# Four small re-timings in a fused encoder layer: early operands one token tile later, first rows in a larger slot, two products on VectorE, and a staggered last product

## The chip, the core and the metric

The kernel runs on one core of a Trainium2 chip. Its five engines are TensorE (PE: matrix products into the banks of PSUM), VectorE (DVE), ScalarE (ACT), GpSimd (POOL) and SyncE (SP, which here issues the DMA transfers). Each engine works through its own queue in order, and a semaphore holds an instruction until what it needs is there. The metric is the time on the device of one execution, in microseconds (us). A measurement of this kernel can tell a difference of about 0.2%, which is 3.6 us.

## What is computed

One layer of a streaming encoder, on 1024 tokens of width 1024 in float32. Two attention branches, a cross-attention to 256 memory tokens and a SwiGLU block follow one another, and each adds its result to the token rows. The change touches the end of the cross-attention and everything behind it:

```python
x = x + memory_cross_attention(hc, mn, w_cq[layer], w_ckv[layer], w_co[layer])
hf = rmsnorm(x, norm_ffn_g[layer])
g, u = jnp.split(hf @ w_gate_up, 2, axis=-1)          # 1024 -> 2 x 2816
x = x + (jax.nn.silu(g) * u) @ w_down                  # 2816 -> 1024
return rmsnorm(x, norm_final_g)
```

## The kernel before

**Arithmetic.** A float32 operand is split into a high part (a cast on ScalarE) and a low part (a subtraction on VectorE); the method `split` of the class does both. Each product is three matmuls: high by high, low by high and high by low (`prod`, or lines 217 to 219 in the part ahead of it).

**Token tiles and rows.** The 1024 tokens are eight tiles of 128. `last_half` takes token tiles 4 to 7 through the output projection of the cross-attention: `add_out` is a group of 12 matmuls and then one VectorE addition to the rows (line 634), twice for each tile, once for each half of the columns; `last_rms` squares and scales the rows (lines 108, 101, 103, 110), and `norms` transposes what the tile before left on TensorE (line 791) and copies it into `hq` (line 794). Between the two groups of tile 4, `ff.before()` starts the SwiGLU block's operands: `mov_early` splits four quarters of the token operand into tiles `T` (lines 894 and 895).

**SwiGLU.** The block multiplies two-by-two blocks of its matrices by a scheme with seven products in place of eight; their order is 1, 2, 6, 5, 7, 3, 4 (`ORDER`). Products 1, 6, 7 and 4 accumulate in bank "a", 2 in "d", and 5 and 3 in "c". The 22 feature tiles of gate (g) and up (u) go in pairs, which gives 154 items of 12 matmuls. Pairs t0 and t1 share the start: items 0 to 7 are products 1 and 2 of t0 g, t0 u, t0 g, t0 u and then the same of t1; items 8 to 17 are products 6, 5, 7, 3 and 4 of t0; items 18 and 19 are product 6 of t1 g and t1 u, which needs t1's bank "a" to have been read. These reads of items 4 to 7 are held back in a list `later` and are flushed after item 17. `make` prepares an item's weights four items ahead (`AHEAD`): on GpSimd sums and differences of weight blocks (lines 956 to 960), then the split. `read` copies a bank into rows `r` (ScalarE, line 989) or adds it to them (VectorE, line 991). `after` adds silu on ScalarE (lines 1021 to 1025) and the products of gate and up rows on GpSimd (line 1029, 128x1024, and line 1033, 128x512).

**Slots.** On-chip tiles come out of rings by tag. A new tile waits until the oldest of its ring is no longer used: "row" has 3 slots of 4 KB for each partition, "sum" 2 of 4 KB, "hidden" and "four" share 8 of 8 KB, "combo" has 3 of 8 KB.

**Down product.** `down` runs 77 steps (7 products by 11 feature pairs), each 12 matmuls: 3 for each of four token tiles. `down_load` asks for a step's operands 8 steps ahead, and `down_make` splits them (`do`) 2 steps ahead. At a product's last step the four banks are added to the rows `xr` (line 1172). At products 3 (steps 55 to 65) and 4 (steps 66 to 76) a row is then complete: two squares on ScalarE (line 1176, both halves of the row), three small operations on GpSimd (lines 1178 to 1180), two scalings on VectorE into `fin` (line 1144), and the output's DMA (line 1146).

The order within an engine's queue is set by a scheduler that works from the program's order and its own estimates, except where `keep_in_program_order` stands.

Of the kernel before, what the change touches and what calls it, by code (L numbers as in the profile page):

```python
# [12 lines left out]
ALU = mybir.AluOpType  # L13
AX = mybir.AxisListType

P = 128
# [21 lines left out]
def build(tc, x, mem, wqk, wv, wg, wup, wout, wcq, wck, wcv, wco, wgu, wdn,  # L38
# [530 lines left out]
    with tc.tile_pool(name="late", bufs=1, reuse_waits="tile") as lt:  # L569
# [66 lines left out]
        def add_out(*a):  # L636
            for _ in out_steps(*a):
                pass
# [175 lines left out]
        def last_half():  # L814

            ws = [[unit(wco[4 + cc + 2 * i], home=t1_tile if cc else None) for i in range(2)] for cc in range(2)]
            for tt in range(4, 8):
                add_out(o_sta(2), ws[0], 4, 0, tt)
                if tt == 4:
                    norms(0)  # L820
                    ff.before()
                add_out(o_sta(2), ws[1], 4, 1, tt)
                norms(0)
                last_rms(tt)

# [39 lines left out]
class FeedForward:  # L865
# [44 lines left out]
        t = self.T[n, i] = self.tiles["hidden"]("T", n)  # L910
        self.split(t[:, 0], t[:, 1], src)

    def mov_early(self):
        for i in (0, 2):
            self.put(1, i, self.quad(i, 0))
        for i in (0, 2):
            self.put(2, i, self.quad(i + 4, 0))

    def mov_late(self, n):

# [17 lines left out]
    class Pair:  # L938
# [38 lines left out]
        def read(self, n):  # L977
            ff = self.ff
            acc = self.bk[ff.BANK[n]]
            if n == 1:  # L980
                self.r = [ff.tiles["sum" if self.f >= FT else "row"]("r"), None]
            elif n == 5:
                self.r[1] = ff.tiles["row"]("r")

            to = {1: (0, 0), 2: (0, 0), 6: (0, 1), 3: (0, 1), 5: (1, 1), 7: (1, 1)}.get(n)
            if to:
                r = self.r[to[0]][:, to[1]]
                if n in (1, 6, 5):
                    ff.act.copy(out=r, in_=acc)  # L989
                else:  # L990
                    ff.dve.tensor_tensor(out=r, in0=r, in1=acc, op=ALU.add)

    class Tile2:
# [19 lines left out]
        def after(self, p, n):  # L1013
            p.read(n)
            g, u, ff = self.g, self.u, self.ff
            act, dve, pool, sp = ff.act, ff.dve, ff.pool, ff.sp
            if p is g:
                if n == 1 and self.f >= 4:
                    self.down_weights()
                elif n == 7:  # L1020
                    act.activation(g.r[1][:, 1], g.r[1][:, 1], AF.Silu)
                elif n == 3:
                    act.activation(g.r[0], g.r[0], AF.Silu)
                elif n == 4:
                    act.activation(g.r[1][:, 0], g.bk["a"], AF.Silu)
            elif n == 7 and self.before:
                self.before.down_weights()
            elif n == 3:
                pool.tensor_tensor(out=g.r[0], in0=g.r[0], in1=u.r[0], op=ALU.mult)
                sp.dma_start(out=ff.a_d[self.f // 2][:, 0:2], in_=g.r[0])  # L1030
            elif n == 4:

                pool.tensor_tensor(out=g.r[1][:, 1], in0=g.r[1][:, 1], in1=u.r[1][:, 1], op=ALU.mult)
                dve.tensor_tensor(out=g.r[1][:, 0], in0=u.bk["a"], in1=g.r[1][:, 0], op=ALU.mult)
                sp.dma_start(out=ff.a_d[self.f // 2][:, 2:4], in_=g.r[1])
                t = ff.tiles["four"]("s")
                (a11, a21), (a12, a22) = ([r[:, 0], r[:, 1]] for r in g.r)
                pool.tensor_tensor(out=t[:, 2], in0=a11, in1=a21, op=ALU.subtract)
                dve.tensor_tensor(out=t[:, 0], in0=a21, in1=a22, op=ALU.add)
                dve.tensor_tensor(out=t[:, 1], in0=t[:, 0], in1=a11, op=ALU.subtract)  # L1040
                dve.tensor_tensor(out=t[:, 3], in0=a12, in1=t[:, 1], op=ALU.subtract)
                sp.dma_start(out=ff.s_d[self.f // 2], in_=t)
# [24 lines left out]
    def before(self):  # L1067

        tiles = []
        for f in range(0, FT, 2):  # L1070
            tiles.append(self.Tile2(self, f, tiles[-2] if f in (4, 6) else None))
        self.items = []
        for ns, ts in ((self.ORDER[:2], tiles[:2]), (self.ORDER[2:], tiles[:2]), (self.ORDER, tiles[2:])):
            for t in ts:
                self.items += t.items(ns)
        self.loaded = []
        self.mov_early()
        for i in range(2):
            self.make(i)

    def run(self, last_norm):
        with self.tc.tile_pool(name="fps", bufs=1, space=bass.MemoryType.PSUM, reuse_waits="tile") as self.fps:
            later = []
            self.steps = [(n, j) for n in self.ORDER for j in range(FT // 2)]
            self.raws, self.ops = {}, {}
            for i in range(2, AHEAD):
                self.make(i)
            for i, (t, p, n) in enumerate(self.items):
                if i == 2:
                    last_norm()  # L1090
                if i in LATE:
                    self.mov_late(LATE[i])
                self.make(i + AHEAD)
                if i == len(self.items) - 9:
                    for k in range(4):
                        self.down_load(k)
                if i == len(self.items) - 2:
                    self.down_make(0)
                p.mm(n)

                if i < 8 and t is self.items[4][0]:
                    later.append((t, p, n))
                else:
                    t.after(p, n)
                if n == 4 and p is t.u:
                    while later:
                        t, p, n = later.pop(0)
                        t.after(p, n)
            self.down()
# [14 lines left out]

    def down_make(self, i):
        if i < len(self.steps):
            t = self.tiles["combo"]("do")
            self.split(t[:, 0], t[:, 1], self.raws[i])
            self.ops[i] = t[:, 0], t[:, 1]

    def down(self):
        act, dve, pool, sp = self.act, self.dve, self.pool, self.sp
        LOADS, MADE = 8, 2
        for i in range(4, LOADS):
            self.down_load(i)
        self.down_make(1)
# [2 lines left out]
        bks = {}  # L1139
        fin = []  # L1140

        def finish(row, o):
            for c in range(2):
                self.tc.keep_in_program_order(dve.scalar_tensor_tensor(
                    out=o[:, c], in0=xs[row][:, c], scalar=sf[:, row, 1:2], in1=gbc[:, c], op0=ALU.mult, op1=ALU.mult))
                sp.dma_start(out=self.out[row * P:(row + 1) * P, c * HALF:(c + 1) * HALF], in_=o[:, c])

        for i, (n, j) in enumerate(self.steps):
            self.down_load(i + LOADS)
            self.down_make(i + MADE)  # L1150
            if i == 4:
# [3 lines left out]
                    xs += [t[:, k].rearrange("p (a b) -> p a b", a=2) for k in range(2)]  # L1155
                gbc = self.tiles["row"]("gbc")
                sp.dma_start(out=gbc, in_=self.g_final.partition_broadcast(P).rearrange("p (a b) -> p a b", a=2))
            b = "a" if self.BANK[n] == "a" else "c"
            first = n in self.FIRST
            if first and j == 0:  # L1160
                bks[b] = [self.bank() for _ in range(4)]
            hi, lo = self.ops.pop(i)
            for tt in range(4):
                ts = slice(tt * P, (tt + 1) * P)
                self.prod(bks[b][tt], (hi[:, 0, ts], lo[:, 0, ts]), (hi[:, 1], lo[:, 1]), first and j == 0,
                          j == FT // 2 - 1, not first)
            if j < FT // 2 - 1:
                continue
            for tt in range(4):
                half, c = {1: (0, 0), 2: (0, 0), 6: (0, 1), 5: (1, 1), 7: (1, 1), 3: (0, 1), 4: (1, 0)}[n]  # L1170
                row = half * 4 + tt
                dve.tensor_tensor(out=xs[row][:, c], in0=xs[row][:, c], in1=bks[b][tt], op=ALU.add)
                if n in (3, 4):
                    o = self.tiles["row"]("fin")
                    for cc in range(2):
                        act.activation(o[:, cc], xs[row][:, cc], AF.Square, accum_out=sf[:, row, cc:cc + 1])
                    s0, s1 = sf[:, row, 0:1], sf[:, row, 1:2]
                    pool.tensor_tensor(out=s1, in0=s0, in1=s1, op=ALU.add)
                    pool.tensor_scalar(out=s1, in0=s1, scalar1=1.0 / D, scalar2=EPS, op0=ALU.mult, op1=ALU.add)
                    pool.tensor_tensor(out=s1, in0=s1, in1=self.mhalf, op=ALU.pow)  # L1180
                    fin.append((row, o))
                    if tt:
                        finish(*fin[-2])
                    if tt == 3:
                        finish(*fin[-1])


def _cols(w, n=128):
# [56 lines left out]
```

## Time and profile before

| | |
|---|---|
| median of 3 runs | 1800.18 us (1797.94 to 1800.35) |
| the profiled execution's own time | 1801.18 us |
| its span, first to last instruction | 1799.4 us |
| TensorE busy | 1745.7 us (97%) |
| mean granted TensorE clock | 0.993 |
| VectorE, ScalarE, GpSimd busy | 1088.5, 766.2, 519.4 us (60%, 43%, 29%) |

The span is the time from the first to the last instruction on the core; 1.8 us of the execution's own time lie around it. Clock 1.00 stands for TensorE's 2.4 GHz, 0.50 for 1.2 GHz. Matmuls overlap one another in the pipeline, so that one of 0.39 us follows the one before at a shorter distance than that.

### The profile page before, as it was taken

To read this page: it belongs to the slowest core of one execution; us is meant where nothing else is said; L and a number is where in the kernel's file an instruction comes from. 1 tells how busy PE (TensorE), PEld (TensorE's weight loads), DVE (VectorE), ACT (ScalarE), POOL (GpSimd) and SP (SyncE) were. 2 spreads that over 40 slices of the span, in tenths; PEclk is the share of its full clock that TensorE was granted. 3 is DMA by queue.
4 is the path that set the end of the run, shared out by engine and by line. 5 is a ranking of instruction groups with operands and counts; after the bars stand their busy time and mean duration, and the time that the engine had idled before them with its cause. 6 is when DMAs were issued, how large, how long until landed. Compare 5 with 4: busy or idle time off the path is not lost.

```text
span 1799.4 us, 23586 instructions
## 1 busy us (share of the span) xinstructions
PE 1745.7 (97%) x8836; PEld 1471.2 (82%) x8836; DVE 1088.5 (60%) x1495; ACT 766.2 (43%) x1425; POOL 519.4 (29%) x555
## 2 busy tenths in 40 slices
PE   7999999999999999999999999989999999999996
PEld 7778797898898888888888887778888888888885
DVE  6585666646756744445645446776676666655555
ACT  5354554535545545213542244343333333334343
POOL 3232213223323202200000001376766656400002
PEclk9999999999999999999999999999999999999998
DMA  5332313212221255421321114225644434586663
GB/s 192 104 90 68 103 42 103 71 54 62 77 74 62 83 219 214 152 72 69 131 104 49 54 63 153 94 87 196 233 177 174 164 141 187 212 286 192 195 192 117
DMA packets 75730, 229.80 MB, mean 128 GB/s; under 512 B 9184, under 2 KB 9440, under 8 KB 71776
## 3 DMA queue, kind: packets, MB, share of 16 engines
q1 hardware_dynamic: 75616, 228.30, 36.7%
q8 instruction: 69, 1.13, 0.3%
q14 instruction: 45, 0.37, 0.1%
HBM read 160.10 MB, written 55.57 MB: 120 GB/s over the span
## 4 chain that ended last, share of the span: by engine, by line
PE 64%; issue 3%; DVE 3%; ACT 1%; POOL 1%; DMA 0%; DVEq 0%; POOLq 0%; ACTq 0%
PE bk L901 11%; PE bk L902 11%; PE bk L900 10%; PE acc L217 5%; PE acc L218 5%; PE acc L219 5%; PE s L95 2%; PE s L96 2%; PE s L97 2%; PE s L217 2%; PE s L219 2%; PE s L218 2%; PE av L454 1%; PE tr L438 1%; PE av L95 0%
## 5 line engine op out<-in xcount | busy, mean ns | idle before, releaser
L217 PE MATMUL acc<-t,wsp 128*128 128x512 f32 (+1 forms) x704 | 270.4, 384 | 0.0
L219 PE MATMUL acc<-t,wsp 128*128 128x512 f32 (+1 forms) x704 | 270.3, 384 | 0.0
L218 PE MATMUL acc<-t,wsp 128*128 128x512 f32 (+1 forms) x704 | 270.2, 384 | 0.0
L900 PE MATMUL bk<-T,w 128*128 128x512 f32 x616 | 240.8, 391 | 5.2 <-ACT r L989 5.0
L901 PE MATMUL bk<-T,w 128*128 128x512 f32 x616 | 240.3, 390 | 1.3 <-DVE w L895 1.3
L902 PE MATMUL bk<-T,w 128*128 128x512 f32 x616 | 240.5, 390 | 0.5 <-DVE T L895 0.5
L895 DVE TENSOR_TENSOR w<-fr,w 128x512 fp32r<-128x512 f32 x132 | 140.8, 1099 | 72.7 <-ACT w L894 72.3
L81 DVE TENSOR_TENSOR wsp<-raw,wsp 128x1024 fp32r<-128x1024 f32 x98 | 124.0, 1265 | 67.5 <-ACT wsp L76 66.2
L219 PEld LDWEIGHTS acc<-t,wsp 128*128 128x128 f32 x704 | 133.3, 189 | 25.1
L76 ACT CAST wsp<-raw 128x1024 fp32r<-128x1024 f32 x96 | 100.7, 1049 | 124.5 <-PE s L219 50.2
L218 PEld LDWEIGHTS acc<-t,wsp 128*128 128x128 f32 x704 | 133.3, 189 | 22.8 <-DVE wsp L81 0.7
L217 PEld LDWEIGHTS acc<-t,wsp 128*128 128x128 f32 x704 | 133.3, 189 | 22.2
L895 DVE TENSOR_TENSOR do<-dr,do 128x1024 fp32r<-128x1024 f32 x77 | 96.8, 1260 | 82.9 <-ACT do L894 81.3
L900 PEld LDWEIGHTS bk<-T,w 128*128 128x128 f32 x616 | 116.1, 188 | 30.2 <-ACT r L989 5.8
L901 PEld LDWEIGHTS bk<-T,w 128*128 128x128 f32 x616 | 116.1, 188 | 25.8 <-DVE w L895 1.7
L902 PEld LDWEIGHTS bk<-T,w 128*128 128x128 f32 x616 | 116.0, 188 | 24.9 <-DVE T L895 0.9
L894 ACT CAST do<-dr 128x1024 fp32r<-128x1024 f32 x77 | 81.2, 1054 | 118.0 <-PE bk L902 103.4
L901 PE MATMUL bk<-do 128*128 128x512 f32 x308 | 120.2, 390 | 0.8 <-DVE do L895 0.8
L902 PE MATMUL bk<-do 128*128 128x512 f32 x308 | 119.9, 389 | 0.0
L900 PE MATMUL bk<-do 128*128 128x512 f32 x308 | 119.7, 389 | 0.0
L217 PE MATMUL acc<-wsp,t 128*128 128x256 f32 (+1 forms) x368 | 118.1, 321 | 1.1 <-POOL wsp L80 1.1
L219 PE MATMUL acc<-wsp,t 128*128 128x256 f32 (+1 forms) x368 | 116.5, 317 | 0.7 <-DVE wsp L81 0.7
(216 smaller groups left out, 3736.8 us busy)
## 6 DMA issues: line engine op xcount, KB each, us to landing
fr<-in_wgu SPq DMA_DIRECT2D x44, 512.0 KB, 5.7
ad<-r SPq DMA_DIRECT2D x22, 512.0 KB, 3.3
sd<-s SPq DMA_DIRECT2D x11, 1024.0 KB, 4.1
dw<-in_wdn SPq DMA_DIRECT2D x22, 512.0 KB, 5.5
wd<-dw SPq DMA_DIRECT2D x11, 1024.0 KB, 4.1
dr<-sd SPq DMA_DIRECT2D x44, 256.0 KB, 3.7
dr<-wd SPq DMA_DIRECT2D x44, 256.0 KB, 3.9
dr<-ad SPq DMA_DIRECT2D x33, 256.0 KB, 5.1
```

The source lines that it names most:

```text
L76: act.copy(out=hi, in_=src)
L81: lo_eng.tensor_tensor(out=lo, in0=src, in1=hi.bitcast(F32), op=ALU.subtract)
L95: pe.matmul(acc, lh, rh, start=(i == 0), stop=False)
L96: pe.matmul(acc, ll, rh, start=False, stop=False)
L217: pe.matmul(acc, lh, rh, start=(i == 0), stop=False)
L218: pe.matmul(acc, ll, rh, start=False, stop=False)
L219: pe.matmul(acc, lh, rl, start=False, stop=(i == n - 1))
L894: self.act.copy(out=hi, in_=src)
L895: self.dve.tensor_tensor(out=lo, in0=src, in1=hi.bitcast(F32), op=ALU.subtract)
L900: mm(acc, l[0], r[0], start=start, stop=False, skip_group_check=onto)
L901: mm(acc, l[1], r[0], start=False, stop=False, skip_group_check=onto)
L902: mm(acc, l[0], r[1], start=False, stop=stop, skip_group_check=onto)
```

## The change

It has four parts. **(1)** `mov_early` is split: product 1's two operand tiles are made where all four were, in `ff.before()`, and product 2's two are made a token tile later, after tile 5's second `add_out`. **(2)** Rows r of pair t1's gate take an 8 KB "four" slot in place of a "row" slot, and the held-back reads of t1 are flushed after item 15 in place of item 17. **(3)** For pair t0 alone the products of lines 1029 and 1033 run on VectorE, not on GpSimd. **(4)** The end of the down product: the last 4 operands come from "hidden" slots (of the ring "t1"), the last 5 steps run token tile by token tile (15 matmuls for a tile, then its row's end) in place of step by step, a half of a row is squared as soon as that half is complete, and the scaled rows overwrite `xr` and leave from there.

```diff
                 add_out(o_sta(2), ws[1], 4, 1, tt)
+                if tt == 5:
+                    ff.mov_early(2)
                 norms(0)
...
-    def mov_early(self):
+    def mov_early(self, n):
         for i in (0, 2):
-            self.put(1, i, self.quad(i, 0))
-        for i in (0, 2):
-            self.put(2, i, self.quad(i + 4, 0))
+            self.put(n, i, self.quad(i + (0 if n == 1 else 4), 0))
...
-                self.r = [ff.tiles["sum" if self.f >= FT else "row"]("r"), None]
+                tile = ff.tiles["four"]("r")[:, :2] if self.f == 2 else ff.tiles["sum" if self.f >= FT else "row"]("r")
+                self.r = [tile, None]
...
-                pool.tensor_tensor(out=g.r[0], in0=g.r[0], in1=u.r[0], op=ALU.mult)
+                (pool if self.f else dve).tensor_tensor(out=g.r[0], in0=g.r[0], in1=u.r[0], op=ALU.mult)
...
-                pool.tensor_tensor(out=g.r[1][:, 1], in0=g.r[1][:, 1], in1=u.r[1][:, 1], op=ALU.mult)
+                (pool if self.f else dve).tensor_tensor(out=g.r[1][:, 1], in0=g.r[1][:, 1], in1=u.r[1][:, 1], op=ALU.mult)
...
-        self.mov_early()
+        self.mov_early(1)
...
-                if n == 4 and p is t.u:
+                if i == 15:
                     while later:
...
-            t = self.tiles["combo"]("do")
+            t = self.tiles["combo"]("do") if i < len(self.steps) - 4 else self.tiles["hidden"]("do", 5)
...
-        LOADS, MADE = 8, 2
+        LOADS, MADE, LAST = 8, 2, 5
...
-        def finish(row, o):
+        def finish(row):
...
-                    out=o[:, c], in0=xs[row][:, c], scalar=sf[:, row, 1:2], in1=gbc[:, c], op0=ALU.mult, op1=ALU.mult))
-                sp.dma_start(out=self.out[row * P:(row + 1) * P, c * HALF:(c + 1) * HALF], in_=o[:, c])
+                    out=xs[row][:, c], in0=xs[row][:, c], scalar=sf[:, row, 1:2], in1=gbc[:, c], op0=ALU.mult, op1=ALU.mult))
+                sp.dma_start(out=self.out[row * P:(row + 1) * P, c * HALF:(c + 1) * HALF], in_=xs[row][:, c])
+
+        def squares(row, c):
+            o = self.tiles["sum"]("fin")
+            act.activation(o[:, c], xs[row][:, c], AF.Square, accum_out=sf[:, row, c:c + 1])
+
+        def add(n, tt):
...
+            dve.tensor_tensor(out=xs[row][:, c], in0=xs[row][:, c], in1=bks[b][tt], op=ALU.add)
+            if n in (2, 7, 3, 4):
+                squares(row, c)
+            if n in (3, 4):
...
+                fin.append(row)
+                if tt:
+                    finish(fin[-2])
+                if tt == 3:
+                    finish(fin[-1])
...
 +        def mm(n, j, tt):
+            bk = bks["a" if self.BANK[n] == "a" else "c"][tt]
+            hi, lo = self.ops[self.ORDER.index(n) * (FT // 2) + j]
+            ts = slice(tt * P, (tt + 1) * P)
+            first = n in self.FIRST
+            self.prod(bk, (hi[:, 0, ts], lo[:, 0, ts]), (hi[:, 1], lo[:, 1]), first and j == 0, j == FT // 2 - 1, not first)
...
         for i, (n, j) in enumerate(self.steps):
+            if i >= len(self.steps) - LAST:
+                break
             self.down_load(i + LOADS)
             self.down_make(i + MADE)
...
+        for k in range(i + MADE, len(self.steps)):
+            self.down_make(k)
+        for tt in range(4):
+            for n, j in self.steps[i:]:
+                mm(n, j, tt)
+            add(n, tt)
```

How the queues change at three places. Lines 894 and 895 of before are 896 and 897 of the change; 989, 991, 1021, 1023, 1025, 1029, 1033, 1038 and 1039 are one higher; 1144, 1146, 1172 and 1176 became 1145, 1147, 1157 and 1151.

VectorE while token tiles 4 and 5 go through the output projection (`T` are the early operands, `xs` the rows, `xn` the normed rows, `hq` the token operand), before:

```order
L895 TENSOR_TENSOR w<-fr,w 128x512
L794 COPY hq<-av 128x4x128
L895 TENSOR_TENSOR T<-hq,T 128x1024 x4
L634 TENSOR_TENSOR xs<-xs,acc 128x512 x2
L110 SCALAR_TENSOR_TENSOR xn<-xs,rstd,gbc 128x1024
L634 TENSOR_TENSOR xs<-xs,acc 128x512
L794 COPY hq<-av 128x4x128
L110 SCALAR_TENSOR_TENSOR xn<-xs,rstd,gbc 128x1024
```

and now:

```order
L897 TENSOR_TENSOR w<-fr,w 128x512
L794 COPY hq<-av 128x4x128
L897 TENSOR_TENSOR T<-hq,T 128x1024 x2
L634 TENSOR_TENSOR xs<-xs,acc 128x512 x2
L897 TENSOR_TENSOR T<-hq,T 128x1024
L110 SCALAR_TENSOR_TENSOR xn<-xs,rstd,gbc 128x1024
L634 TENSOR_TENSOR xs<-xs,acc 128x512
L897 TENSOR_TENSOR T<-hq,T 128x1024
L794 COPY hq<-av 128x4x128
L110 SCALAR_TENSOR_TENSOR xn<-xs,rstd,gbc 128x1024
```

Two of the four `T` now stand behind the two additions to the rows, one of them ahead of the scaling to `xn` and one behind it.

ScalarE from item 11's read to item 19's (`r<-bk` are the copies out of banks, `w` the weights' casts; the lines between are silu), before:

```order
L894 CAST T<-hq 128x1024 x2
L989 COPY r<-bk 128x512
L894 CAST w<-fr 128x512 x2
L1021 ACT_TABLE_LOAD
L1021 ACTIVATE r<-r 128x512
L894 CAST w<-fr 128x512 x2
L989 COPY r<-bk 128x512
L1023 ACTIVATE r<-r 128x1024
L894 CAST w<-s_10972 128x512 x2
L989 COPY r<-bk 128x512
```

and now:

```order
L896 CAST T<-hq 128x1024 x2
L990 COPY r<-bk 128x512 x2
L896 CAST w<-fr 128x512 x2
L1022 ACT_TABLE_LOAD
L1022 ACTIVATE r<-r 128x512
L896 CAST w<-fr 128x512 x2
L1024 ACTIVATE r<-r 128x1024
L896 CAST w<-s_10972 128x512 x2
L990 COPY r<-bk 128x512
L1026 ACTIVATE r<-bk 128x512
```

The copy for item 18 (t1 gate) moved from behind the second `w<-fr` pair to the front. The copy for item 19 (t1 up) stays behind the casts `w<-s`; it waits for VectorE's product of lines 1029 and 1030.

VectorE at the same place, before:

```order
L895 TENSOR_TENSOR w<-fr,w 128x512 x2
L991 TENSOR_TENSOR r<-r,bk 128x512 x2
L895 TENSOR_TENSOR w<-fr,w 128x512 x2
L991 TENSOR_TENSOR r<-r,bk 128x512 x3
L895 TENSOR_TENSOR w<-s_10972,w 128x512 x2
L1039 TENSOR_TENSOR s<-r 128x512
```

and now:

```order
L897 TENSOR_TENSOR w<-fr,w 128x512 x2
L992 TENSOR_TENSOR r<-r,bk 128x512 x3
L1034 TENSOR_TENSOR r<-r 128x512
L897 TENSOR_TENSOR w<-fr,w 128x512 x2
L992 TENSOR_TENSOR r<-r,bk 128x512 x2
L897 TENSOR_TENSOR w<-s_10972,w 128x512
L1030 TENSOR_TENSOR r<-r 128x1024
L897 TENSOR_TENSOR w<-s_10972,w 128x512
L1040 TENSOR_TENSOR s<-r 128x512
L992 TENSOR_TENSOR r<-r,bk 128x512
```

The two products (128x512 and 128x1024) came onto VectorE, the second between the two subtractions `w<-s`. GpSimd's queue lost both.

VectorE where the down product goes from product 3 to product 4 (the first `do` here is step 67's; `xr` are the four rows of product 3), before:

```order
L895 TENSOR_TENSOR do<-dr,do 128x1024
L1172 TENSOR_TENSOR xr<-xr,bk 128x512
L1144 SCALAR_TENSOR_TENSOR fin<-xr,sf,gbc 128x512 x2
L1172 TENSOR_TENSOR xr<-xr,bk 128x512
L1144 SCALAR_TENSOR_TENSOR fin<-xr,sf,gbc 128x512 x2
L1172 TENSOR_TENSOR xr<-xr,bk 128x512
L895 TENSOR_TENSOR do<-dr,do 128x1024 x2
L1144 SCALAR_TENSOR_TENSOR fin<-xr,sf,gbc 128x512 x2
L895 TENSOR_TENSOR do<-dr,do 128x1024
L1144 SCALAR_TENSOR_TENSOR fin<-xr,sf,gbc 128x512 x2
L895 TENSOR_TENSOR do<-dr,do 128x1024 x6
```

and now:

```order
L897 TENSOR_TENSOR do<-dr,do 128x1024
L1157 TENSOR_TENSOR xr<-xr,bk 128x512
L1145 SCALAR_TENSOR_TENSOR xr<-xr,sf,gbc 128x512 x2
L1157 TENSOR_TENSOR xr<-xr,bk 128x512
L1145 SCALAR_TENSOR_TENSOR xr<-xr,sf,gbc 128x512 x2
L1157 TENSOR_TENSOR xr<-xr,bk 128x512
L1145 SCALAR_TENSOR_TENSOR xr<-xr,sf,gbc 128x512 x2
L897 TENSOR_TENSOR do<-dr,do 128x1024
L1145 SCALAR_TENSOR_TENSOR xr<-xr,sf,gbc 128x512 x2
L897 TENSOR_TENSOR do<-dr,do 128x1024 x8
```

Before, steps 68 and 69 stood ahead of the third row's two scalings; now step 68 stands behind three rows' scalings, and step 69 behind all four.

## Rows read from the trace of the kernel before

**Rows 1.** The page's first line
```profile
span 1799.4 us, 23586 instructions
```
**Rows 2.** Windows: us, busy time by engine (x instructions), granted clock, DMA share, GB/s
```profile
1100.00:1150.00 50.00, 45.43 (x216) 36.14 (x215) 34.76 (x40) 23.37 (x37) 10.04 (x18) 0.97 0.43 164
1150.00:1200.00 50.00, 45.75 (x204) 37.10 (x203) 39.67 (x40) 23.82 (x34) 36.44 (x16) 1.00 0.17 63
1200.00:1300.00 100.00, 97.57 (x424) 80.28 (x423) 70.82 (x69) 37.29 (x64) 73.06 (x46) 0.98 0.54 200
1300.00:1750.00 450.00, 450.00 (x1987) 372.75 (x1986) 271.46 (x259) 167.07 (x232) 168.54 (x103) 1.00 0.56 192
1750.00:1800.00 50.00, 34.35 (x148) 27.08 (x146) 28.44 (x35) 19.45 (x38) 10.38 (x24) 0.89 0.34 122
```
**Rows 3.** Timeline of VectorE: start, us, operation, count, idle before it <-its releaser
```profile
1120.70 4.62 DVE L895 TENSOR_TENSOR T<-hq,T 128x1024 fp32r<-128x1024 f32 x4
1125.24 1.28 DVE L634 TENSOR_TENSOR xs<-xs,acc 128x512 f32<-128x512 f32 x2
1128.11 1.28 DVE L110 SCALAR_TENSOR_TENSOR xn<-xs,rstd,gbc 128x1024 f32<-128x1024 f32 x1 [1.59 <-POOL rstd L103]
```
**Rows 4.** Timeline of TensorE at the same place
```profile
1125.97 0.50 PE L217 MATMUL acc<-t,t 128*128 128x512 f32 x1 [2.49 <-DVE xs L634]
...
1130.42 0.60 PE L791 MATMUL tr<-ident,xn 128*128 128x128 f32 x4
```
**Rows 5.** Windows of 2.5 us, columns as in rows 2
```profile
1127.50:1130.00 2.50, 2.50 (x7) 1.97 (x6) 1.28 (x1) 0.00 (x0) 0.55 (x1) 0.50 0.00 0
1205.00:1207.50 2.50, 2.50 (x7) 1.97 (x8) 2.50 (x3) 1.78 (x4) 1.87 (x2) 0.58 0.54 216
```
**Rows 6.** Timeline of GpSimd at pair t0's end
```profile
1174.13 14.97 POOL L956 TENSOR_TENSOR s<-fr 128x512 f32<-128x512 f32 x2 [12.25 <-ACT w L894]
...
1201.80 2.35 POOL L1029 TENSOR_TENSOR r<-r 128x1024 f32<-128x1024 f32 x1 [3.11 <-ACT r L1023]
```
**Rows 7.** Timeline of TensorE at items 18, 19 and 20
```profile
1199.36 0.50 PE L900 MATMUL bk<-T,w 128*128 128x512 f32 x1 [2.52 <-ACT r L989]
...
1204.83 0.50 PE L900 MATMUL bk<-T,w 128*128 128x512 f32 x1 [2.43 <-ACT r L989]
...
1209.27 0.40 PE L900 MATMUL bk<-T,w 128*128 128x512 f32 x1
```
**Rows 8.** Timeline of ScalarE at item 18
```profile
1198.72 0.59 ACT L989 COPY r<-bk 128x512 f32<-128x512 f32 x1 [3.98 <-POOL r L1033]
```
**Rows 9.** Timeline of VectorE before item 18
```profile
1193.53 2.81 DVE L895 TENSOR_TENSOR w<-fr,w 128x512 fp32r<-128x512 f32 x2 [5.64 <-ACT w L894]
```
**Rows 10.** Groups by line, 1600 to 1750 us: busy us, mean ns, idle before
```profile
L895 DVE TENSOR_TENSOR do<-dr,do 128x1024 fp32r<-128x1024 f32 x56 | 68.6, 1224 | 66.8 <-ACT do L894 66.8
L894 ACT CAST do<-dr 128x1024 fp32r<-128x1024 f32 x55 | 58.0, 1055 | 89.8 <-PE bk L902 81.5 <-DVE do L895 6.7 <-issue 1.0
...
L1172 DVE TENSOR_TENSOR xr<-xr,bk 128x512 f32<-128x512 f32 x20 | 12.8, 683 | 5.4 <-PE bk L902 5.4
```
**Rows 11.** Timeline of TensorE at steps 68 and 72
```profile
1758.74 0.61 PE L900 MATMUL bk<-do 128*128 128x512 f32 x2
...
1771.38 0.39 PE L900 MATMUL bk<-do 128*128 128x512 f32 x1
```
**Rows 12.** Timeline of TensorE, its last matmul
```profile
1784.75 0.39 PE L902 MATMUL bk<-do 128*128 128x512 f32 x1
```
**Rows 13.** Timeline of ScalarE after that
```profile
1789.83 0.63 ACT L1176 ACTIVATE fin<-xr 128x512 f32<-128x512 f32 x1 [4.02 <-DMA out_dram<-fin]
...
1791.52 0.63 ACT L1176 ACTIVATE fin<-xr 128x512 f32<-128x512 f32 x1 [0.35 <-DMA out_dram<-fin]
```
**Rows 14.** Timeline of VectorE, its last two products
```profile
1794.52 1.41 DVE L1144 SCALAR_TENSOR_TENSOR fin<-xr,sf,gbc 128x512 f32<-128x512 f32 x2 [0.72 <-POOL sf L1180]
```
**Rows 15.** The page's DMA issues: KB each, median us from issue to landing
```profile
dr<-wd SPq DMA_DIRECT2D x44, 256.0 KB, 3.9
```

More of the change, by code (lines that the diff above doesn't have):

```diff
@@ L1140, in down, with mm @@
         fin = []
-        def finish(row, o):
+        def finish(row):
             for c in range(2):
                 self.tc.keep_in_program_order(dve.scalar_tensor_tensor(
-                    out=o[:, c], in0=xs[row][:, c], scalar=sf[:, row, 1:2], in1=gbc[:, c], op0=ALU.mult, op1=ALU.mult))
-                sp.dma_start(out=self.out[row * P:(row + 1) * P, c * HALF:(c + 1) * HALF], in_=o[:, c])
+                    out=xs[row][:, c], in0=xs[row][:, c], scalar=sf[:, row, 1:2], in1=gbc[:, c], op0=ALU.mult, op1=ALU.mult))
[4 more added lines that the diff above has]
+        def add(n, tt):
+            b = "a" if self.BANK[n] == "a" else "c"
+            half, c = {1: (0, 0), 2: (0, 0), 6: (0, 1), 5: (1, 1), 7: (1, 1), 3: (0, 1), 4: (1, 0)}[n]
+            row = half * 4 + tt
+            dve.tensor_tensor(out=xs[row][:, c], in0=xs[row][:, c], in1=bks[b][tt], op=ALU.add)
+            if n in (2, 7, 3, 4):
+                squares(row, c)
+            if n in (3, 4):
+                s0, s1 = sf[:, row, 0:1], sf[:, row, 1:2]
+                pool.tensor_tensor(out=s1, in0=s0, in1=s1, op=ALU.add)
+                pool.tensor_scalar(out=s1, in0=s1, scalar1=1.0 / D, scalar2=EPS, op0=ALU.mult, op1=ALU.add)
+                pool.tensor_tensor(out=s1, in0=s1, in1=self.mhalf, op=ALU.pow)
+                fin.append(row)
[3 more added lines that the diff above has]
+                    finish(fin[-1])
+        def mm(n, j, tt):
+            bk = bks["a" if self.BANK[n] == "a" else "c"][tt]
[3 more added lines that the diff above has]
+            self.prod(bk, (hi[:, 0, ts], lo[:, 0, ts]), (hi[:, 1], lo[:, 1]), first and j == 0, j == FT // 2 - 1, not first)
         for i, (n, j) in enumerate(self.steps):
+            if i >= len(self.steps) - LAST:
+                break
             self.down_load(i + LOADS)
@@ L1157, in down @@
                 sp.dma_start(out=gbc, in_=self.g_final.partition_broadcast(P).rearrange("p (a b) -> p a b", a=2))
[L1158 to L1162, printed above, removed]
-            for tt in range(4):
[L1164 to L1185, printed above, removed]
+            if n in self.FIRST and j == 0:
+                bks["a" if self.BANK[n] == "a" else "c"] = [self.bank() for _ in range(4)]
+            for tt in range(4):
+                mm(n, j, tt)
+            if j == FT // 2 - 1:
+                for tt in range(4):
+                    add(n, tt)
+        for k in range(i + MADE, len(self.steps)):
+            self.down_make(k)
+        for tt in range(4):
+            for n, j in self.steps[i:]:
+                mm(n, j, tt)
+            add(n, tt)
 def _cols(w, n=128):
```

## The prediction

> **What bounds the kernel now.** The span is 1799.4 us [rows 1]; I read its windows first. From 1300 to 1750 us TensorE is busy for 450.00 of 450.00 us at clock 1.00, with 1987 matmuls, so one matmul costs 450 / 1987 = 0.2265 us and a group of 12 costs 2.72 us [rows 2]. Nothing that is done beside TensorE there can shorten the time. The idle time that the change can reach lies in the other windows: 4.57 us from 1100 to 1150, 4.25 from 1150 to 1200, 2.43 from 1200 to 1300 and 15.65 from 1750 to 1800 [rows 2]. In each of them I then read TensorE's own timeline, took the releaser that stands behind each wait, and followed that one back through the engine that it names. The ends of stretches are counted in groups of 12, since a matmul's own 0.39 us overlap with the next.
>
> **Part 1, the early operands.** VectorE makes four low parts `T` in one run, 4.62 us from 1120.70, so 1.16 each, and only then the two additions to the rows of tile 4 [rows 3]. TensorE waits 2.49 us for them and starts at 1125.97 [rows 4]. Its next 12 matmuls end in the transposes at 1130.42 [rows 4]: 4.45 us in place of 2.72, because the granted clock is 0.50 from 1127.5 to 1130 [rows 5], the lower of the two levels. So this place costs 2.49 + 1.73 = 4.2 us. The total number of operations does not change; two `T` move behind the additions. These then start 2 x 1.16 = 2.3 us earlier, at about 1122.9, and the first ends near 1123.6, with its semaphore some 0.2 later; TensorE could start at 1125.97 − 2.49 = 1123.5 and would wait some 0.4 us. The transposes need `xn`, which is ready at 1129.39 now, 3.5 us after the first addition ends at about 1125.88 (half of the two, which take 1.28) [rows 3]. One `T` now stands ahead of that scaling, but in its wait of 1.59 us [rows 3], so `xn` comes about 1127.4. TensorE gets there at 1123.9 + 2.72 plus a slow start of some 0.2, about 1126.8; it waits 0.6. I count 4.2 − 1.0 = **3.2 us gained**. Bounds: 3.9 if both waits nearly vanish; 1.6 if these waits still cost a clock drop of 1.7. ScalarE's four casts are as they were. Product 2's operands are needed by items 2 and 3, long after.
>
> **Parts 2 and 3, the first rows of t1 and the products.** Item 18 waits 2.52 us for a copy out of its bank and item 19 another 2.43 us [rows 7]. The first copy stood behind GpSimd's line 1033 [rows 8], since its "row" slot was still in use; GpSimd was late because its two sums of line 956 took 14.97 us from 1174.13 [rows 6]. The second stood behind line 1029, 2.35 us from 1201.80 [rows 6]. From item 18's start without a wait, 1199.36 − 2.52 = 1196.84, two groups of 2.72 would put item 20 at 1202.28; it starts at 1209.27 [rows 7]. The place costs 7.0 us, of which 1.7 are the 12 matmuls from 1204.83, with clock 0.58 between 1205 and 1207.5 [rows 5].
>
> In the new order item 18's copy needs no slot of the "row" ring and stands ahead of the last casts, so its wait goes. Item 19's copy still needs a "sum" slot that is given up by the 128x1024 product. That chain I can follow: the weights' low parts `w` end at 1193.53 + 2.81 = 1196.34 [rows 9], and 0.7 later if the 128x512 product on VectorE holds GpSimd up for its own length. Then the addition to the rows (0.68 [rows 10]), the silu (1.06, as a cast of its size [rows 10]), two casts of about 0.56, one low part, the product (1.16, as a `T` of that size [rows 3]) and the copy, 0.59 [rows 8]. On the path lie 1197.0 + 0.7 + 1.1 + 0.5 + 0.7 + 1.2 + 0.6 = 1201.8. Item 19 could start at 1196.84 + 2.72 = 1199.56, so it waits about 2.3 us and picks up slowly (0.3). I count 7.0 − 2.6 = **4.4 us gained**, before any clock drop. Bounds: 5.1 if GpSimd is not held up; 2.0 if that wait grows to 3.0 and the clock drops.
>
> What speaks against the products on VectorE is the starvation of GpSimd: the two sums of line 956 took 14.97 us while VectorE ran without pause, and 1.2 to 1.3 each is what a 128x512 sum takes when it has the memory to itself (half of line 1029's 2.35) [rows 6]. Two more operations on VectorE starve it longer. The Trainium skill's page "GPSIMD Engine Reference", section "Key points", gives a rule for this: GpSimd shares its SBUF interfaces with VectorE and contends with VectorE's instructions that read two SBUF inputs, as both products do. The row of 14.97 us agrees. By the rule alone the 1.9 us of products would delay GpSimd's next sums by as much; here line 1034's share is 0.7, counted above, and the other comes after the weights that item 19 needs.
>
> The move of GpSimd's later weight work goes beside TensorE's 450 us without a gap [rows 2], so I cost it at nothing; so do the squares that move to the ends of products 2 and 7, 0.8 us of ScalarE's time where it sat idle for 89.8 us of 150 [rows 10]. Were a split held up there by more than its lead of two steps, each us would cost one.
>
> **Part 4, the way into product 4.** Before, step 68 starts at 1758.74 and step 72 at 1771.38 [rows 11]: 12.64 us for 48 matmuls that need 10.87, a loss of 1.8. Now step 68's low part stands behind three rows' scalings. Each row costs VectorE 0.68 [rows 10] and 1.41 [rows 14], and its square waits on ScalarE behind a cast of 1.06 [rows 10]. From the end of step 65 (1758.74 less 24 matmuls, 1753.3) I get the third row's scalings at 1759.6 to 1761.0 and step 68's low part at 1762.2 (1.22 [rows 10]). Four of its 12 matmuls need only the high part and go first, until 1759.65; TensorE then waits 2.5 and at step 69 0.3 more. With the slow start after the wait the loss is 3.0: **1.2 us lost**. Bounds 0.4 and 3.
>
> **Part 4, the end.** TensorE ends at 1784.75 + 0.39 = 1785.14 [rows 12], the span at 1799.4 [rows 1]: 14.26 us of row ends, four in a chain, with a 4.02 us wait for an output's DMA to free a `fin` slot [rows 13]. Token tile by token tile, a row's last 15 matmuls take 3.4 us, so that three rows finish under TensorE, and no slot is waited for. After TensorE comes the last addition (0.7), one square (0.8), three small GpSimd operations and two scalings. Before, the last row's two squares start at 1791.52 [rows 13] and its scalings at 1794.52 [rows 14]: 3.0 us, less one square 2.2, which puts GpSimd's part at 1.4. The sum is 0.7 + 0.8 + 1.4 + 1.4 = 4.3, perhaps 5 with the row before beside it, and then 1799.4 − 1795.93 = 3.5 for the last output [rows 1, 14]: 8.3 us. **6.0 us gained**, bounds 5.5 and 6.7.
>
> **The clock.** Of three TensorE waits of 2.43 to 2.52 us, two were followed by a drop to about half (1125.97 and 1204.83) and one was not (1199.36, whose 12 matmuls and wait take 1199.36 to 1204.83, 5.47 us: 2.72 + 2.43 + 0.3) [rows 4, 5, 7]. Two such waits will stand, at item 19 and at step 68. I add one drop, 1.7 us.
>
> **The sum.** −3.2 − 4.4 + 1.2 − 6.0 + 1.7 = −10.7 us. The profiled run took 1801.18, 1.0 over the median of the runs shown; against its own time this is 1790.5, against the median 1789.5. I predict **1789.5 us**.
>
> **Rivals.** *No drop at either place*: −12.4, 1787.8. For it speaks that one of three such waits cost none. *Drops at both*: −9.0, 1791.2. *The stall at item 19 takes back what item 18 saves*, because GpSimd's chain is as late as before (item 18's wait ended with it at 1198.7, 9.6 us behind where line 956 ended): parts 2 and 3 then give only about 0.5, and the sum is −6.8, 1793.4. Against it: item 19 needs no longer GpSimd's product, only its weights. *The end doesn't overlap*: if the row ends still queue behind TensorE, the 6.0 are missing, 1795.5; the order of the queues speaks against it. *Slower*: the last step's operand transfer now stands in SyncE's queue behind 6 and 8 of the first rows' outputs, and is needed about 2.7 us into step 72's group rather than 10.9 us. If the third and fourth rows' outputs come near 1764, it is asked for then, lands 3.9 us later [rows 15] and is split by about 1771; it is needed at about 1775.5. Each us beyond that margin of 4.5 costs one. All gain is gone when it is 15 us late in landing, slower by over 3.6 at 19; at such a delay, 1804. That would take a transfer held back by several rows' ends, and the rows' ends are 1.4 us apart.
>
> **Chances.** Forecast (one drop) 0.36, no drop 0.24, two drops 0.16, item 19's stall 0.12, no overlap at the end 0.04, slower 0.02, and 0.06 for a partial gain in between. The range takes the first four cases with the terms' bounds: 1785 (all at their good ends, −15) to 1795 (item 19's stall with a second drop). Within 0.2% (3.6 us, what a measurement of this kernel can tell) only the no-overlap case with other losses lands: 0.05. Faster by more: 0.93. Slower: 0.02.
>
> **What would show it.** In the profile after: TensorE's wait at 1126 under 1 us and no clock of 0.5 there; no wait at item 18 and one of 2 to 3 us at item 19, its releaser the copy behind VectorE's product; a wait of about 2.5 us within step 68; 8 us between TensorE's last matmul and the span's end. The prediction is wrong if GpSimd's line 956 to 960 end later than 1197.5 in the new order, if `xn` is late for the transposes, or if TensorE waits on the last loads within the last 60 matmuls.

## The result, and the profile after

The changed kernel takes 1788.6 us, median of four runs (1787.55 to 1789.56), against 1799.43 us of before beside it: a ratio of 0.9942, with a 95% interval from 0.9929 to 0.9955, so 10.8 us less. The forecast was 1789.5 us. The profiled execution took 1787.65 us and its span is 1785.8 us.

The windows of the profile after (us, busy time by engine, granted clock, DMA share, GB/s), which answer to [rows 2]:

```profile
1100.00:1150.00 50.00, 47.45 (x234) 37.88 (x233) 36.66 (x43) 25.87 (x42) 13.84 (x20) 1.00 0.48 185
1150.00:1200.00 50.00, 46.32 (x202) 37.37 (x202) 44.39 (x45) 25.92 (x38) 34.70 (x15) 1.00 0.14 53
1200.00:1300.00 100.00, 100.00 (x443) 82.81 (x442) 71.41 (x68) 36.30 (x62) 75.20 (x48) 1.00 0.57 211
1300.00:1735.00 435.00, 435.00 (x1921) 360.20 (x1920) 261.38 (x251) 164.51 (x237) 160.61 (x99) 1.00 0.57 192
1750.00:1786.00 36.00, 25.51 (x110) 20.14 (x109) 21.64 (x26) 8.55 (x15) 7.47 (x17) 0.96 0.34 117
```

Between 1200 and 1300 us TensorE has no idle time left, and the clock of 0.97 and 0.98 in two windows of before has become 1.00. What is still idle lies from 1100 to 1200 and behind 1750. TensorE's own timeline, at the places of [rows 4, 7, 11, 12]:

```profile
1123.53 0.50 PE L217 MATMUL acc<-t,t 128*128 128x512 f32 x1 [0.23 <-DVE xs L634]
...
1127.27 0.66 PE L791 MATMUL tr<-ident,xn 128*128 128x128 f32 x4 [0.23 <-DVE xn L110]
...
1197.99 0.50 PE L902 MATMUL bk<-T,w 128*128 128x512 f32 x1 [1.96 <-ACT r L990]
...
1200.84 0.39 PE L902 MATMUL bk<-T,w 128*128 128x512 f32 x1
...
1750.28 1.07 PE L902 MATMUL bk<-do 128*128 128x512 f32 x4
1753.38 0.50 PE L903 MATMUL bk<-do 128*128 128x512 f32 x1 [2.03 <-DVE do L897]
...
1756.65 0.50 PE L903 MATMUL bk<-do 128*128 128x512 f32 x1 [0.48 <-DVE do L897]
...
1777.63 0.39 PE L904 MATMUL bk<-do 128*128 128x512 f32 x1
```

In place of the 2.49 us at tile 4's rows there are 0.23 there and 0.23 at the transposes, which now follow two matmuls of the next group; item 18's 2.52 us is gone. That of item 19 is still 1.96, and step 68 has a new one of 2.03. Four high-part matmuls go first at step 68 (the x4 at 1750.28), then the row behind them waits. VectorE at the same places:

```profile
1122.79 1.28 DVE L634 TENSOR_TENSOR xs<-xs,acc 128x512 f32<-128x512 f32 x2
...
1125.93 1.28 DVE L110 SCALAR_TENSOR_TENSOR xn<-xs,rstd,gbc 128x1024 f32<-128x1024 f32 x1 [0.72 <-POOL rstd L103]
...
1185.06 1.06 DVE L1034 TENSOR_TENSOR r<-r 128x512 f32<-128x512 f32 x1
...
1196.10 1.22 DVE L1030 TENSOR_TENSOR r<-r 128x1024 f32<-128x1024 f32 x1
...
1750.78 1.41 DVE L1145 SCALAR_TENSOR_TENSOR xr<-xr,sf,gbc 128x512 f32<-128x512 f32 x2 [0.40 <-POOL sf L1164]
1752.11 1.22 DVE L897 TENSOR_TENSOR do<-dr,do 128x1024 fp32r<-128x1024 f32 x1
...
1760.15 4.63 DVE L897 TENSOR_TENSOR do<-dr,do 128x1024 fp32r<-128x1024 f32 x4
...
1781.07 1.41 DVE L1145 SCALAR_TENSOR_TENSOR xr<-xr,sf,gbc 128x512 f32<-128x512 f32 x2 [1.00 <-POOL sf L1164]
```

The additions at 1122.79 stand behind two `T` in place of four; `xn` comes 2.2 us earlier (1125.93 for 1128.11 of [rows 3]). Line 1030, the 128x1024 product, ends at 1197.3, and ScalarE's copy for item 19 comes right behind it. The last scalings end at 1781.07 + 1.41 = 1782.48, and TensorE at 1777.63 + 0.39 = 1778.02: 7.78 us from there to the span's end, against 14.26. ScalarE and GpSimd:

```profile
1180.12 1.07 ACT L990 COPY r<-bk 128x512 f32<-128x512 f32 x2
...
1197.35 0.59 ACT L990 COPY r<-bk 128x512 f32<-128x512 f32 x1 [1.37 <-DVE r L1030]
...
1759.07 1.05 ACT L896 CAST do<-dr 128x1024 fp32r<-128x1024 f32 x1 [2.50 <-DMA dr<-wd]
1760.40 1.05 ACT L896 CAST do<-dr 128x1024 fp32r<-128x1024 f32 x1 [0.28 <-DMA dr<-wd]
```

```profile
1170.60 14.97 POOL L956 TENSOR_TENSOR s<-fr 128x512 f32<-128x512 f32 x2 [12.25 <-ACT w L896]
1185.52 2.99 POOL L957 TENSOR_TENSOR fr<-fr 128x512 f32<-128x512 f32 x2
...
1190.97 3.44 POOL L960 TENSOR_TENSOR fr<-fr 128x512 f32<-128x512 f32 x2
```

The copy for item 18 has moved to 1180.12 (the second of the two) and waits for nothing. GpSimd's two sums take 14.97 us as before. The cast at 1760.40 is that of the last step, 76: it starts as the transfer that SyncE issued last, at 1755.87, has landed, 4.4 us later (the longest of `dr`). The 2.50 us ahead of 1759.07 are named as a transfer's too, but no transfer of `dr` was complete just then. That cast starts as TensorE's step 69 ends (its last matmul ends at 1758.60 + 0.39 = 1758.99), which fits step 72's operand: its slot in the ring of three ("combo") is the one that step 69 gives up.

### The profile page after: what moved, and what is told of

Its sections match the earlier page's. It is cut to its first block, busy times and chain, and to the rows that moved or that the text cites. A ratio compares the mean times of both kernels' runs of the same rounds, so it can differ in the third digit from the quotient of the medians.

```text
span 1785.8 us, 23577 instructions
## 1 busy us (share of the span) xinstructions
PE 1743.1 (98%) x8836; PEld 1469.2 (82%) x8836; DVE 1085.4 (61%) x1497; ACT 765.6 (43%) x1425; POOL 516.0 (29%) x553
## 4 chain that ended last, share of the span: by engine, by line
PE 65%; issue 3%; DVE 3%; ACT 1%; POOL 1%; DMA 1%; DVEq 0%; POOLq 0%; ACTq 0%
PE bk L903 11%; PE bk L904 11%; PE bk L902 11%; PE acc L217 5%; PE acc L218 5%; PE acc L219 5%; PE s L96 2%; PE s L95 2%; PE s L97 2%; PE s L217 2%; PE s L218 2%; PE s L219 2%; PE av L454 1%; PE tr L438 1%; PE av L95 0%
```

## Experiments

All times are medians beside runs of before on the same chip; before was 1799.38 us in the first set, 1798.76 in the second and 1799.7 in the third.

**One part at a time.** The first: part 1 alone.

```diff
...
+                if tt == 5:
+                    ff.mov_early(2)
...
```

> Only part 1: product 2's operands a token tile later. Theory: the wait of 2.49 us for the rows of tile 4 falls to about 0.2 and the low clock behind it goes, so that this place alone gives 3.4 us (1796.0 against 1799.4) and all that follows runs as before, only earlier; items 18 and 19 still wait 2.5 and 2.4 us. Rival: those two waits hang on GpSimd's chain, which does not start earlier when TensorE does, and take the gain back; then items 18 and 19 wait about 3.4 us more in sum and the time stays at 1799.

Measured: 1796.7 us, ratio 0.9983 (0.9974 to 0.9992), 2.7 us less. The interval holds the 3.4. At the place itself TensorE waits 0.20 and 0.27 us, with no low clock behind. What followed was not quite as before. TensorE in this kernel:

```profile
1196.46 0.59 PE L902 MATMUL bk<-T,w 128*128 128x512 f32 x1 [2.51 <-ACT r L989]
1196.85 0.63 PE L903 MATMUL bk<-T,w 128*128 128x512 f32 x1
...
1201.95 0.50 PE L902 MATMUL bk<-T,w 128*128 128x512 f32 x1 [0.88 <-ACT r L989]
```

The low clock (0.63 us a matmul) now lies behind item 18's wait, and item 19 waits only 0.88. From item 18's start to item 19's it is 5.49 us, as in [rows 7] (5.47) where item 18 ran at full clock: item 19's start is set by ScalarE's copy, and a low clock ahead of such a wait costs nothing. The rival, that the waits take the gain back, is wrong: 2.51 and 0.88 us stand against 2.52 and 2.43. So item 20 follows item 19 here after 2.84 us and not after 4.44 as in [rows 7], and this profiled execution lies 4.4 us below that of before, not 2.7.

Parts 2 and 3 alone, and then part 2 without part 3:

```diff
...
-                if n == 4 and p is t.u:
+                if i == 15:
```

> Only parts 2 and 3: t1's first rows in the larger slot, read after item 15, and t0's products on VectorE. Theory: item 18 does not wait, item 19 waits 2.0 us for the copy behind VectorE's product, which gives 4.9 us without a clock drop (1794.5) and 3.2 with one (1796.2). Rival: the products on VectorE starve GpSimd, line 960 ends later by their 1.9 us and item 19 waits 3 us or more: 2.5 us or less gained.

> Part 2 alone: the products of t0 stay on GpSimd. Theory A (the product's engine decides item 19): GpSimd makes the 128x1024 product in 2.35 us against 1.22 on VectorE, behind the 128x512 product and the weights' sums, so item 19 waits 3 to 4 us in place of 2.0, and the kernel is 1.0 to 2.0 us slower than with parts 2 and 3 together. Theory B (the slot and the earlier read do it all): item 19 waits 2.0 to 2.5 us, since the chain's head, the weights and the silu, is the same, and the time is within 0.5 us of parts 2 and 3 together.

Measured: 1796.25 us, ratio 0.9978 (0.9969 to 0.9988), with both; 1797.59, ratio 0.9987 (0.9978 to 0.9996), with the products on GpSimd. In the profile of the first, item 19 waits 1.95 us and a low clock of 7 matmuls follows, which is the case of 3.2 us (3.1 measured):

```profile
1201.62 0.50 PE L900 MATMUL bk<-T,w 128*128 128x512 f32 x1 [1.95 <-ACT r L990]
...
1202.51 0.63 PE L900 MATMUL bk<-T,w 128*128 128x512 f32 x1
```

In the second it waits for GpSimd:

```profile
1201.60 0.58 ACT L990 COPY r<-bk 128x512 f32<-128x512 f32 x1 [2.48 <-POOL r L1030]
```

```profile
1189.11 2.54 POOL L957 TENSOR_TENSOR fr<-fr 128x512 f32<-128x512 f32 x2
...
1197.52 1.29 POOL L1034 TENSOR_TENSOR r<-r 128x512 f32<-128x512 f32 x1
1198.78 2.79 POOL L1030 TENSOR_TENSOR r<-r 128x1024 f32<-128x1024 f32 x1
```

```profile
1202.23 0.80 PE L900 MATMUL bk<-T,w 128*128 128x512 f32 x1 [2.60 <-ACT r L990]
```

2.60 us of wait in place of 1.95: theory B was nearer in the wait. The waits put part 3 at 0.65 us here; the medians differ by 1.3, but their intervals overlap, so a size beyond the waits is not shown. Line 957 (1189.11) takes 2.54 us here, 2.53 or 2.54 in all five profiles where GpSimd makes the 128x512 product, and 2.98 to 3.00 in all seven where line 1034 runs on VectorE beside it: 0.45 us is what GpSimd was held up by that product.

Part 4 alone:

> Only part 4, the end. Theory: 6.5 us less between TensorE's last matmul and the span's end (7.8 in place of 14.3), 1.3 us lost on the way into product 4 (a wait of 2.0 within step 68, 0.5 at step 69): 5.2 us gained, 1794.2. Rival: the loss at step 68 belongs to the one profiled run or is made up for by the last steps, then 6.5 gained, 1792.9. With a clock drop behind the wait at step 68, 3.5 gained, 1795.9.

Measured: 1794.54 us, ratio 0.9972 (0.9962 to 0.9983), 4.8 us less. TensorE waits as in the changed kernel, so the loss belongs to this part:

```profile
1758.88 0.50 PE L901 MATMUL bk<-do 128*128 128x512 f32 x1 [2.12 <-DVE do L895]
...
1762.15 0.50 PE L901 MATMUL bk<-do 128*128 128x512 f32 x1 [0.48 <-DVE do L895]
```

The interval (3.1 to 6.8 us) holds the theory's 5.2, the rival's 6.5 and the 3.5 of a clock drop; the profile decides: the waits are there, no low clock follows, and 7.93 us lie between TensorE's last matmul (1783.18 + 0.39) and the span's end. Items 18 and 19 are still those of before in this kernel, and its profile has the low clock behind item 18, where it is hidden as in part 1 alone: item 19 follows 5.50 us later, item 20 then 2.89.

The three experiments gave 2.7, 3.1 and 4.8 us, 10.6 in sum, and all parts together 10.8; each has an interval of about 2 us to either side.

**The wait at step 68.** The scalings of product 3's rows stand behind steps 68 to 71:

```diff
-                if tt:
+                if n == 4 and tt:
                     finish(fin[-2])
...
+            if i >= len(self.steps) - 9:
+                finish(fin[i - len(self.steps) + 9])
```

> The changed kernel, but the scalings and outputs of product 3's four rows stand one each behind steps 68 to 71 in place of among product 3's last additions, so that steps 68 to 70 are split ahead of them. Theory (step 68 waits because its low part is queued behind three rows' scalings on VectorE): the waits of 2.0 and 0.5 us at steps 68 and 69 go, TensorE ends 2.5 to 3.0 us earlier with the end of 7.8 us as it was, and the kernel is 2 to 3 us faster than the changed one. Rival (step 68 waits for its operand's transfer or for a free slot): the wait stays at 2 us and the time with it.

Measured: 1785.5 us, ratio 0.9925 (0.9913 to 0.9937). VectorE and TensorE:

```profile
1744.46 1.87 DVE L1157 TENSOR_TENSOR xr<-xr,bk 128x512 f32<-128x512 f32 x3
1746.26 3.65 DVE L897 TENSOR_TENSOR do<-dr,do 128x1024 fp32r<-128x1024 f32 x3
1752.50 1.42 DVE L1145 SCALAR_TENSOR_TENSOR xr<-xr,sf,gbc 128x512 f32<-128x512 f32 x2 [2.60 <-POOL sf L1164]
```

```profile
1756.24 0.50 PE L903 MATMUL bk<-do 128*128 128x512 f32 x1 [0.41 <-DVE do L897]
```

Steps 68 to 70 are split at once behind the four rows, the first scaling waits until 1752.50, and steps 68 and 69 wait for nothing; 0.41 us is left, at step 70. The operand was there when the queue let VectorE split it; it was the order in that queue. The medians lie 3.8 us below the changed kernel beside it (1789.27), more than the 2 to 3 that were expected; how much of that is this edit's is read off below.

**The wait at item 19.** t1's first up rows in a row slot:

```diff
-... ff.tiles["sum" if self.f >= FT else "row"]("r")
+... ff.tiles["sum" if self.f >= FT and self.f != FT + 2 else "row"]("r")
```

> The changed kernel, but t1's first up rows take one of the 4 KB row slots that t1's gate no longer uses, in place of the slot that the 128x1024 product gives up. Theory (that slot is item 19's wait): the copy for item 19 runs some 6 us earlier, item 19 does not wait, 2.0 to 2.3 us gained over the changed kernel, and in executions with a low clock behind that wait 1.7 more. Rival (the weights' sums on GpSimd bind items 19 to 21): the wait moves to item 20 or 21 and less than 0.7 us is gained.

Measured: 1785.95 us, ratio 0.9923 (0.991 to 0.9937), 3.3 us below the changed kernel beside it (1789.27). The copy for item 19 now runs with no wait, 5.7 us ahead of 1197.35:

```profile
1191.64 0.58 ACT L990 COPY r<-bk 128x512 f32<-128x512 f32 x1
```

From 1168 us to step 68 no wait above 0.4 us is left on TensorE, and neither item 20 nor item 21 took the wait over.

**Both mends, with and without part 3, and the change again.**

> Both of these mends together. Theory: their gains add, 4 to 5 us less than the changed kernel, near 1784. Rival: one takes the other's place, 2 to 3 us.

> The changed kernel itself again, for comparison on the same chip and for a second look at the clock. Theory (its runs lie in two groups 2 us apart because the clock falls behind the wait at item 19 or within step 68 in some executions and not in others): the profile shows either no low clock behind those waits and a span near 1785.8, or a low clock of 6 to 8 matmuls behind one of them and a span near 1787.5. Rival: the low clock stays away there, and the span differs by what happens in the first 320 us or in one place more.

> Both mends, but t0's products on GpSimd as before the change (part 3 undone). Theory (part 3 was worth something only because item 19's copy waited for the product's slot): with up rows in a row slot nothing on TensorE's path waits for the 128x1024 product; the copy waits for the 128x512 product behind line 960, about 4 us later than with both mends, yet some 2 us ahead of item 19; no wait at items 18 to 21, and the time is that of both mends within 0.5 us. Rival (the products on GpSimd delay the weights of items 20 and 21, or the copy that now waits ahead of the silu does): a wait of 1 to 2 us at item 19, 20 or 21 and 1 to 3.5 us more.

> Both mends again, beside the run without part 3 on the same chip: 1783 to 1784.5, no wait above 0.5 us from item 18 on, no low clock behind item 18.

Both mends: 1783.38 us, ratio 0.9913 (0.9899 to 0.9926), and 1783.14, ratio 0.9911 (0.9897 to 0.9924), in the next set. Together they give 5.9 us over the changed kernel's 1789.27; alone they gave 3.8 and 3.3, 7.1 in sum. The other 1.2 us are not lost: part of the 3.8 lay ahead of anything that an edit touches. TensorE's first matmul behind the rows of tile 4, in the profile of the change again and in that of the scalings moved alone:

```profile
1123.62 0.50 PE L217 MATMUL acc<-t,t 128*128 128x512 f32 x1 [0.21 <-DVE xs L634]
```

```profile
1121.65 0.50 PE L217 MATMUL acc<-t,t 128*128 128x512 f32 x1 [0.23 <-DVE xs L634]
```

No edit touches what runs up to there, and that execution was 1.97 us ahead. Counted from this matmul to the span's end, the profiles take 663.8 us (the change again), 661.9 (scalings moved), 660.2 (up rows in a row slot) and 657.9 (both): 1.9, 3.6 and 5.9 us gained, so the gains add to within 0.4. (The first two of these profiles have a low clock behind item 19, the other two have no wait there.) The change again: 1789.27, ratio 0.9942 (0.9929 to 0.9954). Its profiled execution took 1789.32 us, 1.67 more than the one above, and differs from it at item 19:

```profile
1198.08 0.52 PE L902 MATMUL bk<-T,w 128*128 128x512 f32 x1 [1.96 <-ACT r L990]
...
1200.96 0.63 PE L903 MATMUL bk<-T,w 128*128 128x512 f32 x1
```

The wait is the same 1.96 us, and the low clock follows it this time: item 20 starts 4.43 us after item 19 in place of 2.85, which is 1.58 of the 1.67 us. The changed kernel's nine runs lie at 1787.55 to 1787.92 (four) and at 1789.27 to 1789.56 (five), and the two profiles are one of each group; the median of four, 1788.6, lies between them. That the other seven runs divide for the same reason is likely, but not shown: the part ahead of tile 4 differs by as much from one execution to another.

Without part 3 the mended kernel takes 1787.89 us, ratio 0.9936 (0.9922 to 0.9949), 4.75 us more than with it. The rival was right on the place, and its 1 to 3.5 us were too few:

```profile
1195.84 0.58 ACT L990 COPY r<-bk 128x512 f32<-128x512 f32 x1 [4.01 <-POOL r L1034]
1197.78 1.06 ACT L1024 ACTIVATE r<-r 128x1024 f32<-128x1024 f32 x1 [1.35 <-DVE r L992]
```

```profile
1171.20 14.97 POOL L956 TENSOR_TENSOR s<-fr 128x512 f32<-128x512 f32 x2 [12.24 <-ACT w L896]
...
1198.92 2.36 POOL L1030 TENSOR_TENSOR r<-r 128x1024 f32<-128x1024 f32 x1 [3.11 <-ACT r L1024]
```

```profile
1182.48 1.28 DVE L897 TENSOR_TENSOR w<-fr,w 128x512 fp32r<-128x512 f32 x2
...
1199.38 4.15 DVE L897 TENSOR_TENSOR w<-s,w 128x512 fp32r<-128x512 f32 x2 [1.04 <-ACT w L896]
```

```profile
1201.89 0.50 PE L903 MATMUL bk<-T,w 128*128 128x512 f32 x1 [1.98 <-DVE w L897]
```

The copy for item 19 stands ahead of the silu on ScalarE and waits 4.01 us for GpSimd's 128x512 product; silu and the casts behind it are late, VectorE's two low parts take 4.15 us beside GpSimd's 128x1024 product, where such a pair takes 1.28 at 1182.48, and TensorE waits 1.98 us for the first of them at item 20's second matmul, with a low clock behind. GpSimd was not idle at 1182.48: it was within the two sums that take 14.97 us.

## Why the prediction was right

**The sum.** Each term can be read off as the distance between the same instruction in the two profiles.

| place | forecast | in the profiles |
|---|---|---|
| early operands (item 18 without its wait: 1196.84 to 1197.99 − 1.96 − 2.72 = 1193.31) | −3.2 | −3.5, of which 0.2 had come before it |
| items 18 and 19 (item 20: 1209.27 to 1200.84) | −4.4 | −4.9 |
| way into product 4 (last matmul: 1784.75 to 1777.63, less the above) | +1.2 | +1.3 |
| end (14.26 to 7.78) | −6.0 | −6.5 |
| clock | +1.7 | 0 in this execution, 1.6 in the other |

The profiles differ by 13.6 us of span, the medians by 10.8. Before's profiled execution (1801.18) lay 1.75 above before's median and the change's 0.95 below its own. The single clock drop in the forecast is there in one of the two profiles of the changed kernel, that of 1789.32 us.

The closeness of 1789.5 to 1788.6 is in part luck. The terms together came out 1.3 us larger than forecast (13.6 less 1.6 for the clock is 12.0, for 10.7). The forecast took them off the median of before, which lay 1.0 below the profile from which they were read; the two nearly cancel. And 1788.6 is the middle between two groups of two runs, not a time that a run took.

What was costed at nothing cost nothing: with the squares at the ends of products 2 and 7 and GpSimd's later weight work beside it, TensorE is busy for 435.00 of 435 us (1300 to 1735).

**Part 1.** Waits of 0.23 and 0.23 us in place of 0.4 and 0.6: `xn` was ready at 1125.93 + 1.28 = 1127.2, for 1127.4, and TensorE filled the time with two matmuls. The mechanism was as said.

**Parts 2 and 3.** Item 18 without a wait, item 19 held by the product's slot, 1.96 us for 2.3: the delay of GpSimd by line 1034 was 0.45, not 0.7. The Trainium skill's page "GPSIMD Engine Reference", section "Key points", says that GpSimd contends with VectorE's instructions that read two SBUF inputs, and the rows of 2.54 and 2.99 agree with it. Charging the products' 1.9 us in full would have been four times too much. What I did not see is that part 3 depends on where the copy stands: 0.65 us of wait here, 4.75 us of time once the up rows have their own slot.

**The way into product 4.** Right in size and place (waits of 2.03 and 0.48 us for 2.5 and 0.3); the run with the scalings behind steps 68 to 71 shows that the loss was not needed.

**The clock.** I put a drop behind one of two like waits. The runs showed that they are not alike: behind item 19's wait of 1.95 to 2.6 us a low clock came in five of six profiles that have it, behind step 68's of 1.97 to 2.25 us in none of four. The number was right, the reasoning with two equal places was not.

**The slow rival.** Step 76's operands were nearer to costing time than I said: their transfer landed near 1760.3, ScalarE's cast waited 0.28 us for it (1760.40), and VectorE's split, the last of four in a row, ended at 1760.15 + 4.63 = 1764.78, while TensorE needed them 12 matmuls into the last 60, at about 1777.63 − 47 x 0.2265 = 1767.0. The margin was 2.2 us, not 4.5. With the scalings moved behind steps 68 to 71 it is used up:

```profile
1762.36 2.34 DVE L897 TENSOR_TENSOR do<-dr,do 128x1024 fp32r<-128x1024 f32 x2
```

```profile
1764.76 0.50 PE L903 MATMUL bk<-do 128*128 128x512 f32 x1
```

The split ends at 1764.70 there, and step 76's second matmul starts right behind it.

## What to carry to other kernels

When a wait is on a copy, ask which slot the copy writes and who gives that slot up; here another ring with a free slot gave 3.3 us, and a faster engine for the work that frees the slot 0.65 us of wait. Both still counted together: with the slot free, taking that engine back cost 4.75. When work is added to the end of a product, put it behind the operands of the next one in each queue. Before a clock drop is charged to a wait, see whether the engine waits again directly behind it, since then the slow stretch is hidden there.

## What the runs showed of the hardware

A wait of about 2 us is not enough to say whether TensorE's clock falls from 2.4 to 1.2 GHz: the same 1.96 us at item 19 was followed by a low clock in one execution and not in another. Behind step 68's 1.97 to 2.25 us, where TensorE had run without a gap since about 1200 us, no fall was seen in four profiles. Item 19 has waits of 1.27 and 0.45 us some 30 us ahead of it; tile 4's wait of 2.48 to 2.49 us, which a low clock followed in all four profiles that have it, has waits of 0.44 to 0.70 some 10 us ahead. Whether that is the reason was not tried. VectorE and GpSimd held each other up, and not always in the same direction. While VectorE worked through operation after operation, its pair of low parts took 1.28 us and GpSimd's two sums took 14.97. Where GpSimd's 128x1024 product had begun 0.46 us ahead of such a pair (1198.92 and 1199.38), the product took its 2.36 us and the pair 4.15. That the one which runs first keeps its pace fits both places; no run changed the order alone.
